# One fixed order per engine for the beginning of a hybrid decoder layer, and w_out and the residual loads moved ahead at the end

## The chip, the cores and the metric

The kernel runs on one core of a Trainium2 chip. The metric is the device time of one execution in microseconds (us), here the median of several runs. A core has TensorE (PE in the profile; its weight loads are PEld), VectorE (DVE), ScalarE (ACT), GpSimd (POOL) and SyncE (SP). DMAs are issued from the queues of SP and ACT.

## The reference

One decoder layer on x of shape (1, 1024, 1024), float32. Two token mixers run side by side on the same normalised input and are merged by gates:

```python
h    = rms_norm(x, pre_w)                      # x * rsqrt(mean(x*x) + EPS) * w
proj = h @ w_in                                # 1024 x 6152
sb_qkv, sb_gate, gdn_qkv, gdn_gate, gdn_a, gdn_b, merge_sb, merge_gdn = split(proj)
o_sb = stick_breaking_attention(q, k, v) * silu(sb_gate)        # 8 heads of 64
gdn_qkv = silu(causal_depthwise_conv(gdn_qkv, conv_w))          # 4 taps
o_g  = rms_norm(gated_delta_rule_chunked(q, k, v, g, beta)) * silu(gdn_gate)   # 4 heads of 128
merged = sigmoid(merge_sb) * (o_sb @ w_branch_sb) + sigmoid(merge_gdn) * (o_g @ w_branch_gdn)
y    = merged @ w_out
out  = x + rms_norm(y, post_w)
```

## The kernel before

Tokens are cut into 8 tiles of 128 (`NT`), the model width into 8 blocks of 128 (`NK`), and the tokens also into 4 quarters of 256 (`QT`) and 2 halves of 512 (`HT`). To keep float32 accuracy every large product is made of three matmuls: each operand is split into a rounded part (`hi`, a ScalarE cast) and the rest (`lo`, a DVE subtraction), and hi x hi, hi x lo and lo x hi add up in PSUM (`dense_mm`, L211; `dense`, L221). A weight block is thus loaded to `raw`, cast to `whi` (L88) and subtracted to `wlo` (L89).

The order of the instructions of each engine is set when the program is built: a scheduler takes instructions by their place in the source as they become ready by its own estimate of times, places the semaphores, and gives out buffers. On the chip each engine then works through its queue in that order and waits where an operand isn't there. `tc.issue_after(i)` puts an instruction behind `i` in its engine's queue. `sp` is a pool of 25 slots of 128 x 1024 float32 that nearly all large tiles share (`slot`); a load into a slot waits until the slot's last reader is done.

*Beginning.* SP loads x_0, x_1, the weight block k0, x_2, x_3, block k1, and x_4 to x_7 (L103, L82). For each token tile `stats` squares it with its sum (ScalarE, L183 or L186), takes the root (L154), and DVE makes the reciprocal root with one step of Newton and scales the tile in place (L155 to L160, L188). For each quarter TensorE transposes two tiles into PSUM (`xT`, L274), ScalarE evicts with the norm weight as `h_hi` (L282), DVE as `h_lo` (L283), and the first two weight blocks (k0, k1) are multiplied with that quarter into `pre0` (L211, copied at L294). `keep_awake` issues matmuls of ones as filler. Only the squares are held in order, each behind the root of the tile before, and two of the weight splits; the rest is the scheduler's order. Behind it come the decay and beta logits (`ab`, L307 and L308), the delta-rule mixer and the attention.

*Attention.* `weave` runs one head pair's attention beside the projections of the next pair (for the last pair, beside merge gates), with side work chosen by planned costs. Then `drain(fill(16), att)` issues what is left of both.

*Merge.* The attention outputs are split into hi and lo (L909, L910). For each of 8 blocks m and both halves TensorE makes `d_ya` (12 matmuls of 512 columns), DVE multiplies it by the gate (L948), GpSimd adds the other branch (L949), and `split_m` casts the sum to `m_hi` (ScalarE, L933) and subtracts to `m_lo` (DVE, L934). The gate `sA` and the other branch `mBl` are loaded back from DRAM (L942, L944). In blocks 4 to 7 the first half of w_out is also loaded and split (`rawo`, L918; L924, L925).

*End.* `y` is made for output half n = 0, then n = 1, tile by tile (L977). The second half of w_out is loaded during n = 0. In n = 1 each tile's residual x is loaded again (`xr`, L990), the tile is squared (L981), the root taken, and two scale-and-adds on DVE (L995) are followed by two stores (L996).

Of the kernel before, what the change touches and what calls it, by code (L numbers as in the profile page):

```python
# [26 lines left out]
def tile_stickbreak_gdn_hybrid(  # L27
# [70 lines left out]
    xs = []  # L98
    raw0 = []
    first = [(2560, "k0"), (2688, "k1")]  # L100
    for t in range(NT):
        xt = slot(f"x_{t}")
        nc.sync.dma_start(xt, x2[t * P:(t + 1) * P, :])  # L103
        xs.append(xt)
        if t in (1, 3):
            c0, nm = first[t // 2]
            raw0.append(load_raw(win[:, c0:c0 + P], NK, nm))
    wab = const.tile([P, NK, 8], F32, name="wab")
    nc.scalar.dma_start(wab, win[:, 4096:4104].rearrange("(k p) c -> p k c", p=P))
    alog = const.tile([P, H], F32, name="alog")  # L110
    nc.scalar.dma_start(alog, a_log.broadcast_to([P, H]))
    dtb = const.tile([P, H], F32, name="dtb")
    nc.scalar.dma_start(dtb, dt_bias.broadcast_to([P, H]))
# [60 lines left out]
    prev_sq = [None]  # L174

    def stats(q):
        for j in range(2):
            t = 2 * q + j
            junk = slot(f"xj_{t}")
            ssx = small.tile([P, 1], F32, tag="ssx", name="ssx")  # L180
            rx = small.tile([P, 1], F32, tag="rx", name="rx")
            if prev_sq[0] is None:
                nc.scalar.activation(junk, xs[t], AF.Square, accum_out=ssx)  # L183
            else:
                with tc.issue_after(prev_sq[0].ins):
                    nc.scalar.activation(junk, xs[t], AF.Square, accum_out=ssx)  # L186
            prev_sq[0] = rsqrt_act(rx, ssx, 1.0 / D, epsb, EPS)
            last = nc.vector.tensor_scalar(xs[t], xs[t], rx, None, op0=ALU.mult)  # L188
        return last

    sc0 = stats(0)
    behind = [(prev_sq[0], sc0)]

    par_ps = gps("par_ps")
    nc.tensor.transpose(par_ps[:, :57], stage, ident[:57, :57])
    par = const.tile([P, 57], F32, name="par")
    with tc.issue_after(sc0.ins):
        nc.vector.tensor_copy(par, par_ps[:, :57])
# [65 lines left out]
    w0 = []  # L264
    pre0 = [slot("pre_k0"), slot("pre_k1")]
    for q in range(4):
        if q < 3:
            stats(q + 1)
        for k2 in range(NK // 2):
            ps = gps(f"xT_{q}_{k2}")  # L270
            for kk in range(2):
                for j in range(2):
                    k = k2 * 2 + kk
                    xt_ = nc.tensor.transpose(ps[:, (kk * 2 + j) * P:(kk * 2 + j + 1) * P],  # L274
                                        xs[2 * q + j][:, k * P:(k + 1) * P], ident)
            if q == 0 and k2 % 2:
                keep_awake(6, xt_)
            qs = slice(q * QT, (q + 1) * QT)
            for kk in range(2):
                k = k2 * 2 + kk  # L280
                pk = ps[:, kk * QT:(kk + 1) * QT]
                ev = nc.scalar.mul(h_hi[:, k, qs], pk, prew[:, k:k + 1])  # L282
                lo_ = nc.vector.scalar_tensor_tensor(h_lo[:, k, qs], pk, prew[:, k:k + 1],  # L283
                                                     h_hi[:, k, qs].bitcast(F32), op0=ALU.mult, op1=ALU.subtract)
        if q < 2:
            act_, dve_ = behind[q]
            with tc.issue_after(act_.ins), tc.issue_after(dve_.ins):
                w0.append(split_w(raw0[q], NK, first[q][1]))
            behind.append((ev, lo_))
        todo = [(0, q)] if q < 2 else ([(1, 0), (1, 1), (0, 2), (1, 2)] if q == 2 else [(0, q), (1, q)])  # L290
        for i, qq in todo:
            ps = psd.tile([P, QT], F32, tag="d", name=f"d_{first[i][1]}_{qq}")
            dense_mm(ps, w0[i], NK, hk, qq * QT, (qq + 1) * QT)
            nc.scalar.copy(pre0[i][:, qq * QT:(qq + 1) * QT], ps)  # L294
# [604 lines left out]
    for p in range(NP):  # L899
        side = chain(*[f(p + 1) for f in stages], fill(1)) if p + 1 < NP else fill(4)  # L900
        weave(until_none(att), 24.0, side, 52.0 if p + 1 < NP else 41.0)
    drain(fill(16), att)


    os_hi, os_lo = [], []
    for p in range(NP):
        hi = slot(f"oshi_{p}", F32R)
        lo = slot(f"oslo_{p}", F32R)
        nc.scalar.copy(hi, osb[p])  # L909
        nc.vector.tensor_sub(lo, osb[p], hi.bitcast(F32))  # L910
        os_hi.append(hi)
        os_lo.append(lo)
# [15 lines left out]

    m_hi = big.tile([P, NK, T], F32R, tag="big", name="m_hi")
# [7 lines left out]
    for m in range(NK):  # L937
        wb = load_w(w_branch_sb[0][:, m * P:(m + 1) * P], 4, f"wbs{m}")
        if m >= 4:
            rw = load_wo(0, m - 4)  # L940
# [12 lines left out]
        if m >= 4:  # L953
            split_wo(0, m - 4, rw)
# [6 lines left out]
    ys, sy0 = [], [None] * NT  # L961
    for n in range(2):
        ns = slice(n * HT, (n + 1) * HT)
        for t in range(NT):
            ts_ = slice(t * P, (t + 1) * P)
            if n == 0:
                if t % 2 == 0:
                    split_wo(1, t // 2, load_wo(1, t // 2))
                ys.append(slot(f"y_{t}"))
            y = ys[t]  # L970
# [18 lines left out]
            xt = slot(f"xr_{t}")  # L989
            nc.sync.dma_start(xt, x2[ts_, :])  # L990
            ry = small.tile([P, 1], F32, tag="ry", name="ry")
            rsqrt_act(ry, ss, 1.0 / D, sy0[t], sy0[t])
            for m in range(2):
                ms = slice(m * HT, (m + 1) * HT)
                nc.vector.scalar_tensor_tensor(y[:, ms], y[:, ms], ry, xt[:, ms], op0=ALU.mult, op1=ALU.add)  # L995
                nc.sync.dma_start(out2[ts_, ms], y[:, ms])  # L996
# [28 lines left out]
```

## Time and profile before

| what | us |
|---|---|
| median of 3 runs | 953.26 (953.21 to 953.89) |
| the profiled execution | 953.58 |
| its span, first to last instruction | 951.8 |
| TensorE busy | 924.6 (97%) |
| DVE busy | 591.0 (62%) |
| ScalarE busy | 384.9 (40%) |
| GpSimd busy | 166.4 (17%) |

Times in the rows are from the span's start. A timeline row has the start, the duration, engine, line, operation, what is written from what, and a count; where a row merges several instructions the duration runs from the first to the last. In square brackets stands how long the engine was idle before it and what released it.

### The profile page before, as it was taken

The page shows a single profiled execution, that of the slowest core. Times are in us where ns is not written, and L with a number is a line of the kernel's source. Part 1 is how long each engine was busy: PE and PEld are TensorE (multiplying, and loading weights), DVE is VectorE, ACT ScalarE, POOL GpSimd, SP SyncE. Part 2 cuts the span into 40 slices and gives each one's busy share as a digit, 9 for nine tenths or more (in the row PEclk, how much of TensorE's full clock was granted, in tenths as well). Part 3 has the DMA queues.
Part 4 walks back from the last instruction along what each step waited for, and adds up shares of the span by engine and source line. Part 5 has one row for each costly group of instructions (what it writes and reads, how often), then busy time and mean ns, then how long its engine had stood idle before and what let it go on. Part 6 is the DMA issues. An engine that isn't in the chain of part 4 may idle for free.

```text
span 951.8 us, 13464 instructions
## 1 busy us (share of the span) xinstructions
PE 924.6 (97%) x5194; PEld 760.5 (80%) x5194; DVE 591.0 (62%) x1066; ACT 384.9 (40%) x861; POOL 166.4 (17%) x113
## 2 busy tenths in 40 slices
PE   8999999999999999999999999999999999989995
PEld 7978888788787888887888788887877877768884
DVE  5669895366999834655576445763774664653244
ACT  6666431145554122442354234543453443232211
POOL 1021210001113000000143112431431450440000
PEclk9999999999999999999999999999999999999998
DMA  7014214300232331006620111121102113761054
GB/s 253 16 45 122 78 67 133 67 23 23 67 78 74 127 93 41 12 12 232 222 67 23 45 54 36 27 64 26 42 23 89 34 40 128 254 232 45 22 177 155
DMA packets 88419, 80.13 MB, mean 84 GB/s; under 512 B 17097, under 2 KB 74530, under 8 KB 88354
## 3 DMA queue, kind: packets, MB, share of 16 engines
q1 hardware_dynamic: 86944, 79.20, 27.0%
q8 instruction: 41, 0.67, 0.3%
q10 hardware_dynamic: 1410, 0.07, 0.1%
q14 instruction: 24, 0.20, 0.1%
HBM read 60.88 MB, written 18.37 MB: 83 GB/s over the span
## 4 chain that ended last, share of the span: by engine, by line
PE 81%; DVE 9%; DMA 4%; ACT 2%; issue 2%; POOL 2%; SPq 0%; DVEq 0%; POOLq 0%; ACTq 0%
PE d_mg L221 17%; PE y L977 6%; PE d_sk L221 5%; PE d_sv L221 5%; PE d_gg L221 5%; PE d_sgt L221 5%; PE d_yb L221 4%; PE d_sq L221 4%; PE d_v L221 4%; PE av L832 4%; PE aT L819 3%; PE d_k L221 2%; PE d_k L211 2%; DMA xr<-in_x_dram 2%; PE z L796 2%
## 5 line engine op out<-in xcount | busy, mean ns | idle before, releaser
L803 POOL TENSOR_TENSOR bt<-bt,kp 128x127 f32<-128x127 f32 (+3 forms) x64 | 102.6, 1613 | 380.6 <-DMA mb<-mg_d 155.4
L802 DVE TENSOR_TENSOR_SCAN kp<-kp,mscan 128x128 f32<-128x128 f32 (+3 forms) x64 | 103.8, 1640 | 26.3 <-ACT kp L799 26.0
L221 PE MATMUL d_mg<-h_hi,whi_mg 128*128 128x512 f32 x256 | 101.5, 396 | 1.0 <-ACT mg L676 1.0
L221 PE MATMUL d_mg<-h_lo,whi_mg 128*128 128x512 f32 x256 | 99.9, 390 | 0.0
L221 PE MATMUL d_mg<-h_hi,wlo_mg 128*128 128x512 f32 x256 | 99.8, 390 | 0.0
L799 ACT ACTIVATE kp<-z 128x384 f32<-128x384 f32 (+4 forms) x96 | 48.5, 505 | 44.3 <-PE z L797 41.5
L221 PEld LDWEIGHTS d_mg<-h_hi,whi_mg 128*128 128x128 f32 x256 | 48.1, 188 | 12.5 <-issue 1.7
L221 PEld LDWEIGHTS d_mg<-h_hi,wlo_mg 128*128 128x128 f32 x256 | 48.1, 188 | 10.2
L221 PEld LDWEIGHTS d_mg<-h_lo,whi_mg 128*128 128x128 f32 x256 | 48.1, 188 | 9.3
L977 PE MATMUL y<-wohi,m_hi 128*128 128x512 f32 (+1 forms) x136 | 51.3, 377 | 0.5 <-ACT m_hi L933 0.5
L977 PE MATMUL y<-wohi,m_lo 128*128 128x512 f32 (+1 forms) x136 | 51.3, 377 | 0.0
L977 PE MATMUL y<-wolo,m_hi 128*128 128x512 f32 (+1 forms) x136 | 51.2, 377 | 0.0
L800 ACT ACTIVATE bt<-z 128x384 f32<-128x384 f32 (+4 forms) x96 | 49.1, 512 | 2.1 <-DMA mB_d<-mb 1.7
L369 POOL TENSOR_TENSOR acc_k<-acc_k,pre_k 128x1024 f32<-128x1024 f32 x4 | 9.6, 2390 | 166.0 <-ACT pre_k L368 166.0
L832 PE MATMUL av<-aT,svn 128*64 128x256 f32 (+1 forms) x320 | 36.8, 366 | 1.1 <-DVE aT L825 1.1
L819 PE MATMUL aT<-ident,bt 128*128 128x128 f32 x288 | 36.5, 273 | 0.0
L89 DVE TENSOR_TENSOR wlo_mg<-raw_mg,whi_mg 128x1024 fp32r<-128x1024 f32 x16 | 24.6, 1535 | 18.7 <-ACT whi_mg L88 18.6
L819 PEld LDWEIGHTS aT<-ident,bt 128*128 128x128 f32 x288 | 32.9, 140 | 3.4 <-issue 0.2
L949 POOL TENSOR_TENSOR sA<-sA,mBl 128x512 f32<-128x512 f32 x16 | 26.2, 1643 | 51.6 <-DVE sA L948 49.5
L981 ACT ACTIVATE yj<-y 128x512 f32<-128x512 f32 (+1 forms) x17 | 9.7, 573 | 61.9 <-PE y L977 53.8
L832 PEld LDWEIGHTS av<-aT,svn 128*64 128x64 f32 x320 | 20.7, 136 | 15.8 <-issue 4.9
L676 ACT ACTIVATE mg<-d_mg 128x512 f32<-128x512 f32 x32 | 19.1, 602 | 31.0 <-PE d_mg L221 28.3
(379 smaller groups left out, 2446.8 us busy)
## 6 DMA issues: line engine op xcount, KB each, us to landing
raw_mg<-in_w_in_dram SPq DMA_DIRECT2D x16, 512.0 KB, 4.4
mg_d<-mg SPq DMA_DIRECT2D x16, 512.0 KB, 3.0
x<-in_x_dram SPq DMA_DIRECT2D x8, 512.0 KB, 6.9
mb<-mg_d SPq DMA_DIRECT2D x8, 512.0 KB, 6.2
mB_d<-mb SPq DMA_DIRECT2D x8, 512.0 KB, 3.7
sA<-mg_d SPq DMA_DIRECT2D x8, 512.0 KB, 5.8
mBl<-mB_d SPq DMA_DIRECT2D x8, 512.0 KB, 5.4
rawo<-in_w_out_dram SPq DMA_DIRECT2D x8, 512.0 KB, 6.7
```

Source lines behind the costliest of these rows:

```text
L89: nc.vector.tensor_sub(lo[:, :nk], raw[:, :nk], hi[:, :nk].bitcast(F32))
L211: nc.tensor.matmul(ps, lhsT=a[:, k], rhs=b[:, c0:c1], start=(k == 0 and i == 0), stop=(k == nk - 1 and i == 2))
L221: nc.tensor.matmul(ps, lhsT=a[:, k], rhs=b[:, hs], start=(k == 0 and i == 0), stop=(k == nk - 1 and i == 2))
L676: nc.scalar.activation(gt[:, hs], ps, AF.Sigmoid)
L799: nc.scalar.activation(kp[:, os_], ps[:, :pc], AF.Sigmoid, scale=-0.125)
L800: nc.scalar.activation(bt[:, os_], ps[:, :pc], AF.Sigmoid, scale=0.125)
L802: nc.vector.tensor_tensor_scan(kp[:, :n], kp[:, :n], mscan[:, :n], 1.0, op0=ALU.mult, op1=ALU.max)
L803: nc.gpsimd.tensor_tensor(bt[:, 1:n], bt[:, 1:n], kp[:, 0:n - 1], op=ALU.mult)
L819: nc.tensor.transpose(ps[:, (a * 2 + j) * P:(a * 2 + j + 1) * P], at[p, a, qb][:, off:off + P], ident)
L832: nc.tensor.matmul(av[a * 64:(a + 1) * 64, j0 * P:2 * P], lhsT=vn[:, c, a * 64:(a + 1) * 64], rhs=aT[:, a * 2 + j0:a * 2 + 2], start=(c == ...
L949: nc.gpsimd.tensor_tensor(ga[:, hs], ga[:, hs], mb[:, hs], op=ALU.add)
L977: nc.tensor.matmul(ps, lhsT=a[:, k, ts_], rhs=b[:, c0:c1], start=(k == 0 and i == 0), stop=(k == NK - 1 and i == 2))
```

## The change

It has four parts.

1. The loads at the start: x_2 is issued on ScalarE's queue, x_3 and k1 follow on SP, and wab, alog and dtb go from ScalarE's queue to SP's, behind x_7.
2. The beginning gets one order for each of ScalarE and DVE: `queued` puts every instruction behind the last one given to that engine. The statistics are cut into a ScalarE part (`stat_act`) and a DVE part (`stat_dve`), and so are the splits of k0 and k1. Squares of tiles 3 to 7 come behind evictions of h: the tiles of the next quarter are squared and scaled between the evictions of this one. k0 and k1 are multiplied with every quarter in turn. One of two bursts of filler among the first transposes is dropped.
3. The first half of w_out is loaded and split ahead of `drain(fill(16), att)` instead of in blocks 4 to 7 of the merge.
4. In the end the residual tile t + 4 is loaded when tile t of n = 1 begins, and the very last store goes through ScalarE's queue.

The core of the diff:

```diff
-    for t in range(NT):
-        xt = slot(f"x_{t}")
-        nc.sync.dma_start(xt, x2[t * P:(t + 1) * P, :])
-        xs.append(xt)
-        if t in (1, 3):
-            c0, nm = first[t // 2]
-            raw0.append(load_raw(win[:, c0:c0 + P], NK, nm))
+    load_tile(0, nc.sync)
+    load_tile(1, nc.sync)
+    load_first(0, nc.sync)
+    load_tile(2, nc.scalar)
+    load_tile(3, nc.sync)
+    load_first(1, nc.sync)
+    for t in range(4, NT):
+        load_tile(t, nc.sync)
...
-    nc.scalar.dma_start(wab, win[:, 4096:4104].rearrange("(k p) c -> p k c", p=P))
+    nc.sync.dma_start(wab, win[:, 4096:4104].rearrange("(k p) c -> p k c", p=P))
...
+    def queued(eng, f):
+        with ExitStack() as held:
+            if eng in tail:
+                held.enter_context(tc.issue_after(tail[eng].ins))
+            tail[eng] = f()
...
+    def stat_act(t):
+        junk = slot(f"xj_{t}")
+        ssx[t] = const.tile([P, 1], F32, name=f"ssx_{t}")
+        rx[t] = const.tile([P, 1], F32, name=f"rx_{t}")
+        queued("act", lambda: nc.scalar.activation(junk, xs[t], AF.Square, accum_out=ssx[t]))
+        queued("act", lambda: nc.scalar.activation(rx[t], ssx[t], AF.Sqrt, scale=1.0 / D, bias=epsb))
...
+    stat_act(0)
+    stat_act(1)
+    split_act(0)
+    stat_act(2)
+    stat_dve(0)
...
+    queued("dve", lambda: nc.vector.tensor_copy(par, par_ps[:, :57]))
+    stat_dve(1)
+    split_dve(0)
...
-            if q == 0 and k2 % 2:
+            if q == 0 and k2 == NK // 2 - 1:
                 keep_awake(6, xt_)
...
+    def x_h(q, banks, k):
+        qs = slice(q * QT, (q + 1) * QT)
+        pk = banks[k // 2][:, (k % 2) * QT:(k % 2 + 1) * QT]
+        queued("act", lambda: nc.scalar.mul(h_hi[:, k, qs], pk, prew[:, k:k + 1]))
+        queued("dve", lambda: nc.vector.scalar_tensor_tensor(h_lo[:, k, qs], pk, prew[:, k:k + 1],
+                                                             h_hi[:, k, qs].bitcast(F32),
+                                                             op0=ALU.mult, op1=ALU.subtract))
...
+    for q in range(4):
+        banks = x_t(q)
+        for k in range(NK):
+            x_h(q, banks, k)
+            if q < 3 and k == 2:
+                if q:
+                    stat_act(2 * q + 2)
+                stat_dve(2 * q + 2)
+            if q < 3 and k == 4:
+                stat_act(2 * q + 3)
+            if q < 3 and k == 5:
+                stat_dve(2 * q + 3)
+        if q == 0:
+            split_act(1)
+            split_dve(1)
+        first_d(0, q)
+        first_d(1, q)
...
+    for k2 in range(4):
+        split_wo(0, k2, load_wo(0, k2))
     drain(fill(16), att)
...
-        if m >= 4:
-            rw = load_wo(0, m - 4)
...
-        if m >= 4:
-            split_wo(0, m - 4, rw)
...
+    def load_x(upto):
+        for t in range(len(xr), min(upto, NT)):
+            xt = slot(f"xr_{t}")
+            nc.sync.dma_start(xt, x2[t * P:(t + 1) * P, :])
+            xr.append(xt)
...
+            else:
+                load_x(t + 4)
...
-            xt = slot(f"xr_{t}")
-            nc.sync.dma_start(xt, x2[ts_, :])
+            xt = xr[t]
...
-                nc.sync.dma_start(out2[ts_, ms], y[:, ms])
+                (nc.scalar if last and m else nc.sync).dma_start(out2[ts_, ms], y[:, ms])
```

`stat_dve` holds the six DVE instructions of one tile's statistics in the order of before (scaled sum, reciprocal, three of the Newton step, the scaling of the tile), `x_t` the 16 transposes of a quarter, `first_d` the 24 matmuls of one block with one quarter and the copy of the result.

## Rows read from the trace of the kernel before

**Rows 1.** The page: busy time of each engine with its share of the span and its instructions, and the chain that ended last by engine.

```profile
PE 924.6 (97%) x5194; PEld 760.5 (80%) x5194; DVE 591.0 (62%) x1066; ACT 384.9 (40%) x861; POOL 166.4 (17%) x113
...
PE 81%; DVE 9%; DMA 4%; ACT 2%; issue 2%; POOL 2%; SPq 0%; DVEq 0%; POOLq 0%; ACTq 0%
```

**Rows 2.** The table by stretch: from and to, length, busy us of TensorE, of its weight loads, of DVE, ScalarE and GpSimd (each with its count), the granted TensorE clock as a share of full speed, the busy share of the DMA engines, and GB/s.

```profile
14.30:22.30 8.00, 6.51 (x40) 5.06 (x40) 6.42 (x18) 5.85 (x14) 0.00 (x0) 1.00 0.67 236
22.30:46.60 24.30, 24.26 (x201) 23.95 (x202) 15.97 (x49) 16.09 (x42) 0.00 (x0) 1.00 0.08 23
46.60:801.70 755.10, 749.73 (x4278) 612.20 (x4276) 493.38 (x849) 318.29 (x718) 136.17 (x80) 1.00 0.24 69
801.70:856.90 55.20, 49.78 (x214) 39.43 (x214) 34.64 (x43) 17.55 (x27) 24.01 (x15) 1.00 0.59 215
...
940.10:951.80 11.70, 0.00 (x0) 0.00 (x0) 3.89 (x10) 0.77 (x3) 0.00 (x0) 0.65 0.45 161
```

**Rows 3.** The chain that ended last, in order of time: start, us, what.

```profile
4.59 5.87 DMA x<-in_x_dram
...
30.60 8.16 PE d_k L211 x68
38.76 1.75 PE xT L274 x16
...
943.64 3.69 DMA xr<-in_x_dram
```

**Rows 4.** The timeline of TensorE, at 22 us, at 46 us and at the first tile of y.

```profile
22.32 0.39 PE L211 MATMUL d_k<-h_hi,whi_k 128*128 128x256 f32 x1 [0.35 <-ACT h_hi L282]
...
46.43 0.40 PE L307 MATMUL ab<-h_hi,wab_r 128*16 128x512 f32 x1
...
856.89 0.50 PE L977 MATMUL y<-wohi,m_hi 128*128 128x512 f32 x1 [0.55 <-ACT m_hi L933]
```

**Rows 5.** The timeline of ScalarE and of DVE in the beginning.

```profile
4.63 1.06 ACT L183 ACTIVATE xj<-x 128x1024 f32<-128x1024 f32 x1 [1.71 <-DMA x<-in_x_dram]
6.01 1.04 ACT L186 ACTIVATE xj<-x 128x1024 f32<-128x1024 f32 x1
...
11.60 1.03 ACT L88 CAST whi_k<-raw_k 128x1024 fp32r<-128x1024 f32 x1
13.78 0.45 ACT L282 ACTIVATE h_hi<-xT,par 128x256 fp32r<-128x256 f32 x1
...
6.13 0.16 DVE L156 RECIPROCAL rx<-rx 128x1 f32<-128x1 f32 x1 [0.17 <-ACT rx L154]
7.70 0.15 DVE L156 RECIPROCAL rx<-rx 128x1 f32<-128x1 f32 x1
...
39.74 2.93 DVE L283 SCALAR_TENSOR_TENSOR h_lo<-xT,par,h_hi 128x256 fp32r<-128x256 f32 x7 [5.15 <-ACT h_hi L282]
```

**Rows 6.** What TensorE waited for in the whole span: us in total, times, longest.

```profile
PE d_ya L221 <- DVE wlo_wbs L89: 3.8, 2, 1.9
```

**Rows 7.** The timeline of DVE and GpSimd in the merge stage: the first and the last multiply (L948), one add beside wlo_wbs, and one turn of the loop.

```profile
806.42 0.69 DVE L948 TENSOR_TENSOR sA<-sA,d_ya 128x512 f32<-128x512 f32 x1 [0.94 <-PE d_ya L221]
...
821.99 1.67 POOL L949 TENSOR_TENSOR sA<-sA,mBl 128x512 f32<-128x512 f32 x1 [2.06 <-DVE sA L948]
...
832.59 0.68 DVE L948 TENSOR_TENSOR sA<-sA,d_ya 128x512 f32<-128x512 f32 x1
833.40 1.28 POOL L949 TENSOR_TENSOR sA<-sA,mBl 128x512 f32<-128x512 f32 x1 [2.11 <-DVE sA L948]
835.37 0.69 DVE L934 TENSOR_TENSOR m_lo<-sA,m_hi 128x512 fp32r<-128x512 f32 x1 [2.10 <-ACT m_hi L933]
835.98 0.68 DVE L948 TENSOR_TENSOR sA<-sA,d_ya 128x512 f32<-128x512 f32 x1
836.58 1.22 DVE L925 TENSOR_TENSOR wolo<-rawo,wohi 128x1024 fp32r<-128x1024 f32 x1
836.74 2.17 POOL L949 TENSOR_TENSOR sA<-sA,mBl 128x512 f32<-128x512 f32 x1 [2.06 <-DVE sA L948]
...
857.48 0.68 DVE L948 TENSOR_TENSOR sA<-sA,d_ya 128x512 f32<-128x512 f32 x1
```

**Rows 8.** The timeline of ScalarE and DVE behind the last matmul.

```profile
940.41 0.19 ACT L981 ACTIVATION_READ_ACCUMULATOR yj<-y 128x1 f32 x1
...
943.10 0.42 DVE L986 TENSOR_TENSOR y<-y,postw 128x256 f32<-128x256 f32 x1
944.19 0.16 DVE L160 TENSOR_TENSOR ry<-ry,rat 128x1 f32<-128x1 f32 x1
947.42 1.42 DVE L995 SCALAR_TENSOR_TENSOR y<-y,ry,xr 128x512 f32<-128x512 f32 x2 [3.07 <-DMA xr<-in_x_dram]
```

**Rows 9.** What the DMA engines moved from 0 to 24 us, in 40 equal slices of 0.6 us.

```profile
GB/s 0 0 6 178 177 348 389 431 358 333 314 216 81 111 314 424 396 379 351 344 332 383 403 403 410 423 403 403 394 339 317 258 130 3 0 0 0 23 125 253
```

**Rows 10.** The loads of k0 and k1: issue durations in ns, first and last start in us, and us from issue to landing.

```profile
L82 SPq DMA_DIRECT2D raw_k<-in_w_in_dram x2: 426/430/433, 1.7 to 6.3; - x2
...
DMA to landing us min/median/max: 6.3/6.3/6.3
```

**Rows 11.** The table by stretch, with the columns of rows 2, ahead of the merge stage.

```profile
784.30:794.50 10.20, 10.20 (x50) 8.10 (x50) 0.04 (x1) 1.22 (x3) 0.00 (x0) 1.00 0.25 79
794.50:801.70 7.20, 7.20 (x69) 5.68 (x65) 6.45 (x10) 5.09 (x7) 0.00 (x0) 1.00 0.79 287
```

## What the change was predicted to do

> **What bounds the kernel now.** The page comes first: TensorE is busy for 97% of the span, and 81% of the chain that ended last runs through it [rows 1]. So a change pays only where TensorE stands still or does filler. The table by stretch says where that is [rows 2]. From 22.3 to 46.6 us it is busy for 24.26 of 24.30 us, and from 46.6 to 801.7 us for all but 5.4 of 755 us. Three stretches are left, and they are those that the diff edits: the first 22 us, 801.7 to 856.9 us (5.4 us idle), and the 11.7 us behind the last matmul.
>
> *The beginning.* TensorE's useful work before 22.32 us is 32 transposes and 24 matmuls of 256 columns. By long runs in the chain (16 transposes in 1.75 us, so 0.11 us each; 68 matmuls in 8.16 us, so 0.12 us each [rows 3]) that is 3.5 + 2.9 = 6.4 us of 22.3. From 22.32 us to the first `ab` matmul at 46.43 us it runs through [rows 4]. The chain shows why it starts late: x_2 is issued at 4.59 us, when x_0 has landed, and lands 5.87 us later, at 10.46 [rows 3]; behind it ScalarE squares it, casts whi_k0, squares x_3, and only at 13.78 us evicts the first h_hi [rows 5].
>
> *The merge stage (L936 to L956).* Two TensorE waits of 1.9 us are put down to wlo_wbs [rows 6]. But TensorE is not alone there. For each half of a block DVE multiplies, GpSimd adds, ScalarE casts and DVE subtracts, and DVE's queue has that subtraction ahead of the next multiply. So a half is a loop of four steps: multiply at 832.59 us, add at 833.40, subtract at 835.37 when the cast is there, next multiply at 835.98, together 3.39 us [rows 7]. TensorE, with 214 matmuls in 49.78 busy us [rows 2], needs 12 x 0.233 = 2.8 us for a half. Its last wait there, at 856.89 us, is for m_hi, the loop's product [rows 4].
>
> *The end.* xr_7 is issued at 943.64 us and takes 3.69 us [rows 3]; the last two scale-and-adds start at 947.42 us, waiting for it, though their factor ry was ready at 944.19 + 0.16 = 944.35 [rows 8].
>
> **The change part by part.** The sum is made against the profiled execution, 953.58 us (its span of 951.8 us and 1.8 around it); the median shown is 953.26.
>
> *Loads at the start.* x_2 moves to ScalarE's DMA queue; wab, alog and dtb move behind x_7 on SP, and their first readers stand behind the last h_hi. Fewer loads are then issued ahead of x_2 and x_3, so they need not wait for x_0 and x_1 to land. The transfers themselves hardly gain: 314 to 431 GB/s move in nearly every slice from 3 to 18 us, with one dip to 216, 81 and 111 GB/s between 6.6 and 8.4 us [rows 9], which the small loads moved away would leave. x_2 now runs beside x_1 and k0. 512 KB at about 400 GB/s are 1.3 us, so k0, which is issued at 1.7 us and lands 6.3 later, at 8.0 [rows 10], comes at 8.0 (the dip that goes pays for x_2) to 9.3 us (it does not).
> The Trainium skill, *DMA: Bandwidth & Descriptors*, section "Issuing engines are not separate DMA queues", speaks against this edit: DMAs from any engine's queue run interleaved on the same 16 DMA engines, and a second issuing engine saves only issue time. By that rule alone k0 comes at the late end, 9.3 us, and the sum below would be 0.7 us worse.
>
> *One order.* ScalarE's queue is now: squares 0 and 1, cast whi_k0, square 2, then the eight h_hi, with square 3 behind the fifth. From k0's landing it takes the cast 1.03, a square with its root 6.01 - 4.63 = 1.38, and h_hi 0.45 [rows 5], together 2.9 us: first h_lo at 10.9 us, or 12.2 with the late k0, or 12.3 if x_2 comes no earlier than 10.46 us. I take 11.5. From there DVE's queue holds 8 h_lo of (2.93 - 0.47)/6 = 0.41 us, two statistics of 7.70 - 6.13 = 1.57 us [rows 5] and the subtraction wlo_k1, 1.2 us like that of wolo [rows 7]: 3.3 + 3.1 + 1.2 = 7.6 us, so wlo_k1 is done at 19.1 us (18.5 to 19.9). By then TensorE has done what it had done at 22.32 us, 24 matmuls and 32 transposes, with the same 168 and 32 left. That is 3.2 us won (2.4 to 3.8). Behind it DVE needs 3.3 + 3.1 = 6.4 us a quarter and TensorE 16 x 0.11 + 48 x 0.12 = 7.5, so TensorE paces; but the last two h_lo of a quarter stand behind a statistic, for which I allow 0.5 us (0 to 1.5). **Beginning: 2.7 us won (0.9 to 3.8).** What follows shifts whole, since TensorE has no idle in the 24 us behind it and 5.4 in the next 755 [rows 2]. The dropped filler (6 of 12 keep-awake matmuls among the transposes) costs nothing while the clock holds; else it is a rival below.
>
> *w_out ahead.* Four loads, four casts and four subtractions of 1.22 us [rows 7] leave the merge stage and go behind the last attention weave. They are free if they come before 794.5 us: of the 10.2 us from 784.3 on DVE is busy 0.04 and ScalarE 1.22 [rows 11]. From 794.5 to 801.7 us DVE is busy 6.45 of 7.2 us [rows 11], and all four subtractions there cost up to 4 x 1.22 = 4.9 us. The 12 tiles need slots of the 25; I count 11 held at 785 us (4 bt, svn, 4 osb, up to 2 gates), so they fit. In the merge stage the waits for wlo_wbs (3.8 us [rows 6]) can go, yet the loop of four stays: an add beside wolo takes 2.17 us, one beside nothing 1.28, and one beside wlo_wbs alone 1.67 (at 821.99 us) [rows 7], so a removed wolo gives about 0.5 us, for three of them 1.5. **Merge: 1.5 us won.** Bounds: every half by the loop, with the slower add in every second, is 15 x (3.39 + 0.2) = 53.9 us against 857.48 - 806.42 = 51.1 from first to last multiply [rows 7], 2.8 lost; TensorE alone pacing, 5.4 won, its idle there [rows 2]. I lean to the loop: nothing in the diff reorders it.
>
> *Residual loads ahead.* xr_7 is issued with tile 4 instead of behind the stores of tile 6. ScalarE's last read ends at 940.41 + 0.19 = 940.60 us; from the multiply by postw to ry's end it is 943.10 to 944.35, 1.25 us; so the scale-and-adds start at 940.65 + 1.25 = 941.9 instead of 947.42 us [rows 8]. **End: 5.5 us won** (5.0 to 5.7). The cover is three tiles of matmuls between load and use; slots are free, since the first half of w_out ends with the last matmul of n = 0. The last store on ScalarE's queue gains nothing by itself: its half is ready 0.7 us behind the other's.
>
> Sum: 953.58 - 2.7 - 1.5 - 5.5 = **943.9 us**.
>
> **The rivals.**
> *The beginning gives nothing.* The fixed queues wait in order, so a late k0 or x_3 holds every eviction behind it, and an order of TensorE's that puts k1's matmuls ahead of the next transposes would leave DVE idle. For it: two whole engines are chained. Against it: the loads move at 400 GB/s and end by 19 us [rows 9], ahead of their turn. Time: 953.6 - 1.5 - 5.5 = 946.6.
> *The clock falls.* In its first 8 us of real work TensorE gets transposes, one burst of filler, and then matmuls at DVE's pace. At half rate the 24 matmuls and 16 transposes cost 2.9 + 1.8 = 4.7 us more: 948.6. Against it: the clock was 1.00 through the same sparse stretch, 14.30 to 22.30 us [rows 2], though with two bursts ahead.
> The Trainium skill, *TensorE: Matmul & The Clock Gate*, section "Part 4: PE-mode transpose", says that transposes do not count as the array's activity in the way matmuls do; by that rule this rival gains, and no row here separates the two.
> *The merge stage opens.* If the new order has the next multiply ahead of the subtraction, TensorE paces: 943.9 - (5.4 - 1.5) = 940.0.
> *Slower: SP's queue blocks.* If 12 slots are free only when the last bt are transposed (about 798 us), the four w_out loads stand at the head of SP's in-order queue, and mg_d, raw_wbs, sA and mBl wait behind them: 4 x 1.3 us of transfers, then four subtractions in the busy stretch, 5.2 + 4.9 = 10.1 us, against 2.7 + 5.5 won elsewhere: 955.5. It decides once the loads are issued after about 796 us; issued by 788 they cost nothing. Against it: the last weave has no next head pair to prepare, which frees some 8 slots.
> *The subtractions alone in the busy stretch:* 943.9 + 4.9 = 948.8.
>
> **How the numbers follow.** Chances: forecast 0.62; beginning gives nothing 0.10; clock 0.06; merge opens 0.08; subtractions late 0.09; SP blocks 0.05. The forecast's own range by its bounds is 940 to 947.5; to leave out no more than 2 in 10 the range goes on to the 948.8 above and to an opened merge stage with the beginning's better end below: 939 to 949. The three runs of this kernel lie within 0.1%, so 0.2% (1.9 us) is about what can be told from no change. Faster 0.93, within 0.2% 0.03, slower 0.04.
>
> **What would show it.** The first `ab` matmul near 43.7 us (now 46.43), the first d_k matmul near 11.5 us, and no 3 us wait for x_2's square; in the merge stage no wlo_wbs waits, but m_hi still the last to release y; no DMA wait at L995, and the last scale-and-adds less than 2 us behind the last matmul. The prediction is wrong if the 755 us between are scheduled anew with much more than their 5.4 us of idle, or if the w_out splits stand between 794 and 806 us.

## The result and the profile after

The change makes the kernel slower: 960.85 us (median of 4 runs, 959.19 to 961.49) against 953.56 (median of 4 runs beside them, 953.21 to 953.89), a ratio of 1.0079 with a 95% interval of 1.0066 to 1.0092. The forecast was 943.9, with a range of 939 to 949. The span of the profiled execution is 959.2 us, 7.4 more than before. TensorE's starts divide it like this (us; "last z" is the last score matmul of the attention):

| stretch | before | after | difference |
|---|---|---|---|
| start to first `ab` | 46.43 | 50.38 | +3.95 |
| to the first d_mg behind the last z | 728.07 | 729.91 | +1.84 |
| to the first d_ya (attention tail) | 27.12 | 35.62 | +8.50 |
| to the first y (merge stage) | 49.80 | 48.38 | -1.42 |
| to the last matmul | 88.35 | 88.29 | -0.06 |
| to the end | 12.08 | 6.63 | -5.45 |

The page of after, as [rows 1], and the table by stretch, with the columns of [rows 2]:

```profile
PE 930.6 (97%) x5182; PEld 762.2 (79%) x5182; DVE 589.0 (61%) x1066; ACT 385.7 (40%) x861; POOL 166.0 (17%) x113
PE 83%; DVE 8%; ACT 3%; issue 2%; DMA 2%; POOL 1%; SPq 0%; ACTq 0%; DVEq 0%; POOLq 0%
```
```profile
22.40:50.40 28.00, 25.43 (x197) 23.48 (x198) 16.28 (x49) 16.60 (x42) 0.00 (x0) 1.00 0.07 20
50.40:788.00 737.60, 731.98 (x4158) 597.94 (x4155) 486.06 (x838) 312.15 (x709) 137.85 (x80) 1.00 0.23 68
...
800.60:815.90 15.30, 9.45 (x64) 6.97 (x62) 9.34 (x12) 7.05 (x10) 0.00 (x0) 0.78 0.35 115
815.90:864.30 48.40, 45.22 (x195) 35.52 (x193) 25.67 (x36) 13.31 (x21) 19.85 (x13) 1.00 0.62 220
```

From 22.4 us to `ab`, where TensorE had no idle time before, it has 2.6 us; from 800.6 to 815.9 us it is busy for 9.45 of 15.3 us, and part of that at a lower clock.

*The attention tail.* What TensorE waited for from 788 to 816 us, then ScalarE's timeline, then that of SP's queue, and what SP's queue waited for from 776 to 804 us:

```profile
PE aT L869 <- ACT aT L877: 5.9, 1, 5.9
```
```profile
789.79 1.04 ACT L960 CAST wohi<-rawo 128x1024 fp32r<-128x1024 f32 x1
795.88 1.05 ACT L960 CAST wohi<-rawo 128x1024 fp32r<-128x1024 f32 x1 [5.05 <-DMA rawo<-in_w_out_dram]
...
800.19 1.04 ACT L960 CAST wohi<-rawo 128x1024 fp32r<-128x1024 f32 x1
806.29 1.04 ACT L960 CAST wohi<-rawo 128x1024 fp32r<-128x1024 f32 x1 [5.05 <-DMA rawo<-in_w_out_dram]
807.24 1.08 ACT L726 ACTIVATE mg<-d_mg 128x512 f32<-128x512 f32 x2
808.21 1.08 ACT L877 COPY aT<-aT 128x512 f32<-128x512 f32 x2
```
```profile
775.83 0.45 SPq L954 DMA_DIRECT2D rawo<-in_w_out_dram  x1
789.92 0.34 SPq L727 DMA_DIRECT2D mg_d<-mg  x1
790.36 0.38 SPq L82 DMA_DIRECT2D raw_wbs<-in_w_branch_sb_dram  x1
790.79 1.51 SPq L954 DMA_DIRECT2D rawo<-in_w_out_dram  x2
801.04 0.37 SPq L82 DMA_DIRECT2D raw_wbs<-in_w_branch_sb_dram  x1
801.50 1.64 SPq L954 DMA_DIRECT2D rawo<-in_w_out_dram  x1
```
```profile
SPq L727 <- ACT mg L726: 13.6, 1, 13.6
SPq L82 <- DVE sgT L889: 9.0, 1, 9.0
SPq L954 <- PE aT L869: 1.5, 1, 1.5
```

The four loads do not go out together. In SP's queue the second and third stand behind the store of a merge gate (`mg_d`), which waits 13.6 us for ScalarE's sigmoid, until 789.92 us. The fourth stands behind the load of raw_wbs, which waits some 9 us for DVE, until 801.04; its own slot costs it 1.5 us more (for TensorE's transposes of a bt), so that it leaves at 803.0. Its cast stands in ScalarE's queue ahead of two sigmoids of mg and the copies of aT, so ScalarE stands for 5.05 us and TensorE for 5.9. Behind that wait TensorE runs at half its clock (1.2 GHz) for 6.8 us; the table by stretch before, during and behind it:

```profile
789.00:802.70 13.70, 13.70 (x75) 11.23 (x74) 5.31 (x6) 4.45 (x6) 0.00 (x0) 1.00 0.45 143
802.70:807.10 4.40, 0.29 (x3) 0.05 (x1) 0.00 (x0) 0.81 (x1) 0.00 (x0) 1.00 0.47 155
807.10:813.90 6.80, 5.05 (x24) 3.59 (x26) 6.07 (x8) 5.60 (x9) 0.00 (x0) 0.50 0.19 77
```

5.05 busy us at half the clock are 2.5 more than at the full one (an estimate); with the wait of 5.9 that is 8.4 of the 8.50.

*The beginning.* The first d_k comes at 12.26 us instead of 14.28, 0.8 later than the forecast 11.5. Then ScalarE and DVE wait for each other. Their timelines at the end of the beginning, and one row of ScalarE in the kernel before:

```profile
44.30 0.85 ACT L317 ACTIVATE h_hi<-xT,par 128x256 fp32r<-128x256 f32 x2
45.74 0.84 ACT L317 ACTIVATE h_hi<-xT,par 128x256 fp32r<-128x256 f32 x2 [0.58 <-DVE h_lo L318]
```
```profile
44.83 0.88 DVE L318 SCALAR_TENSOR_TENSOR h_lo<-xT,par,h_hi 128x256 fp32r<-128x256 f32 x2 [1.31 <-ACT h_hi L317]
46.25 0.88 DVE L318 SCALAR_TENSOR_TENSOR h_lo<-xT,par,h_hi 128x256 fp32r<-128x256 f32 x2 [0.54 <-ACT h_hi L317]
```
```profile
42.70 0.47 ACT L282 ACTIVATE h_hi<-xT,par 128x256 fp32r<-128x256 f32 x1 [0.66 <-DVE h_lo L283]
```

A pair of columns takes 1.42 us (44.83 to 46.25), 0.71 a column; before, seven h_lo ran back to back at 0.41 [rows 5]. Two columns share a PSUM bank, one of the separate blocks of PSUM, in which a quarter's transposes land, and the h_hi of a bank's second column waits 0.58 us for DVE's h_lo of its first. The kernel before had the same wait: 0.66 us at 42.70 us, where two columns of one bank came in turn. The Trainium skill, *PSUM — Partial Sum Buffer*, section "PSUM bank collisions raise a hardware error", has a rule that accounts for it: two engines must not access one bank at once, reads against reads included, and the compiler back end's scheduler puts a dependency between them. The trace agrees, with the 0.58 us.

*The merge stage and the end.* DVE at two turns of the loop, and DVE behind the last matmul:

```profile
848.43 0.68 DVE L998 TENSOR_TENSOR sA<-sA,d_ya 128x512 f32<-128x512 f32 x1
...
851.55 0.69 DVE L986 TENSOR_TENSOR m_lo<-sA,m_hi 128x512 fp32r<-128x512 f32 x1 [1.84 <-ACT m_hi L985]
852.16 0.68 DVE L998 TENSOR_TENSOR sA<-sA,d_ya 128x512 f32<-128x512 f32 x1
854.95 0.69 DVE L986 TENSOR_TENSOR m_lo<-sA,m_hi 128x512 fp32r<-128x512 f32 x1 [2.11 <-ACT m_hi L985]
855.56 0.68 DVE L998 TENSOR_TENSOR sA<-sA,d_ya 128x512 f32<-128x512 f32 x1
...
954.54 0.16 DVE L168 TENSOR_TENSOR ry<-ry,rat 128x1 f32<-128x1 f32 x1
954.73 1.41 DVE L1051 SCALAR_TENSOR_TENSOR y<-y,ry,xr 128x512 f32<-128x512 f32 x2
```

The loop of four steps is still there, 3.40 us from multiply to multiply [rows 7]. What went are the slow turns: those with a subtraction of w_out took 4.23 us before (835.98 to 840.21 us), and such a turn takes 3.73 now (848.43 to 852.16). At the end the scale-and-adds follow ry without the DMA wait of [rows 8].

### The profile page after: what moved, and what is told of

Same layout as the page of the kernel before. It is cut to its first block, busy times and chain, and to the rows that moved or that the text cites. A ratio compares the mean times of both kernels' runs of the same rounds, so it can differ in the third digit from the quotient of the medians.

```text
span 959.2 us, 13456 instructions
## 1 busy us (share of the span) xinstructions
PE 930.6 (97%) x5182; PEld 762.2 (79%) x5182; DVE 589.0 (61%) x1066; ACT 385.7 (40%) x861; POOL 166.0 (17%) x113
## 4 chain that ended last, share of the span: by engine, by line
PE 83%; DVE 8%; ACT 3%; issue 2%; DMA 2%; POOL 1%; SPq 0%; ACTq 0%; DVEq 0%; POOLq 0%
PE d_mg L255 17%; PE y L1034 8%; PE d_sk L255 5%; PE d_sv L255 5%; PE d_gg L255 5%; PE d_sgt L255 5%; PE d_yb L255 4%; PE d_v L255 4%; PE d_sq L255 4%; PE av L882 4%; PE aT L869 3%; PE d_k L255 2%; PE d_ya L255 2%; PE z L846 2%; PE z L847 2%
## 5 line engine op out<-in xcount | busy, mean ns | idle before, releaser
L853 POOL TENSOR_TENSOR bt<-bt,kp 128x127 f32<-128x127 f32 (+3 forms) x64 | 104.7, 1646 | 378.6 <-DMA mb<-mg_d 155.4
L255 PEld LDWEIGHTS d_mg<-h_hi,wlo_mg 128*128 128x128 f32 x256 | 48.0, 188 | 10.2
L999 POOL TENSOR_TENSOR sA<-sA,mBl 128x512 f32<-128x512 f32 x16 | 23.7, 1482 | 60.2 <-DVE sA L998 60.2
L1034 PEld LDWEIGHTS y<-wohi,m_hi 128*128 128x128 f32 x136 | 25.6, 188 | 7.1 <-DVE sA L998 1.7
```

The lines of the kernel that those rows point to most:

```text
L255: nc.tensor.matmul(ps, lhsT=a[:, k], rhs=b[:, hs], start=(k == 0 and i == 0), stop=(k == nk - 1 and i == 2))
L853: nc.gpsimd.tensor_tensor(bt[:, 1:n], bt[:, 1:n], kp[:, 0:n - 1], op=ALU.mult)
L999: nc.gpsimd.tensor_tensor(ga[:, hs], ga[:, hs], mb[:, hs], op=ALU.add)
L1034: nc.tensor.matmul(ps, lhsT=a[:, k, ts_], rhs=b[:, c0:c1], start=(k == 0 and i == 0), stop=(k == NK - 1 and i == 2))
```

## The experiments

Each run stands beside runs of the kernel before (medians 953.2 to 953.9 us). "Tail" is from the first d_mg behind the last z to the first d_ya, "merge" from there to the first y; the expectations of u_wo and u_split_late count the tail from a later d_mg (19.4 us where this count has 27.1). All ratios are to the kernel before.

| kernel | us | ratio, 95% interval | first d_k | first ab | tail | merge |
|---|---|---|---|---|---|---|
| before | 953.56 | | 14.28 | 46.43 | 27.12 | 49.80 |
| after | 960.85 | 1.0079 (1.0066 to 1.0092) | 12.26 | 50.38 | 35.62 | 48.38 |
| u_wo | 952.17 | 0.9985 (0.9976 to 0.9994) | 12.29 | 50.25 | 27.11 | 49.87 |
| u_split_late | 952.86 | 0.9988 (0.9978 to 0.9997) | 12.55 | 50.64 | 27.12 | 49.46 |
| u_two | 950.81 | 0.9974 (0.9960 to 0.9987) | 12.82 | 50.13 | 27.11 | 49.27 |
| u_bank | 955.94 | 1.0030 (1.0019 to 1.0042) | 12.05 | 46.43 | 35.78 | 48.38 |
| u_bank_stat | 956.15 | 1.0024 (1.0013 to 1.0035) | 12.14 | 45.52 | 35.41 | 48.38 |
| u_wo_free | 956.74 | 1.0037 (1.0023 to 1.0052) | 23.59 | 53.90 | 27.12 | 50.73 |
| b_end | 949.22 | 0.9947 (0.9931 to 0.9964) | 15.40 | 48.69 | 27.12 | 50.13 |
| u_wo_merge | 947.22 | 0.9933 (0.9913 to 0.9952) | 12.92 | 51.03 | 27.11 | 43.84 |
| b_end_merge | 942.48 | 0.9887 (0.9872 to 0.9901) | 14.28 | 46.39 | 27.12 | 43.82 |
| u_best | 941.39 | 0.9877 (0.9854 to 0.9901) | 12.99 | 46.39 | 27.12 | 43.83 |
| u_best_two | 942.47 | 0.9886 (0.9871 to 0.9901) | 12.34 | 46.55 | 27.11 | 43.75 |
| u_best_sp | 941.02 | 0.9869 (0.9854 to 0.9883) | 12.42 | 44.82 | 27.11 | 43.86 |

**The attention tail: u_wo, u_split_late, u_two.** First the whole part undone, then only its casts and subtractions put back, then half of it.

```
u_wo: loads and splits in the merge stage again
-    for k2 in range(4):
-        split_wo(0, k2, load_wo(0, k2))
...
+        if m >= 4:
+            rw = load_wo(0, m - 4)
...
+        if m >= 4:
+            split_wo(0, m - 4, rw)
u_split_late: loads as in the change, splits in the merge stage
-    for k2 in range(4):
-        split_wo(0, k2, load_wo(0, k2))
+    rws = [load_wo(0, k2) for k2 in range(4)]
...
+        if m >= 4:
+            split_wo(0, m - 4, rws[m - 4])
u_two: two blocks behind the weave, two in merge blocks 6 and 7 as in u_wo
-    for k2 in range(4):
+    for k2 in range(2):
```

> The changed kernel with only the w_out part undone: the four loads and splits of the first half of w_out stand in merge blocks 4 to 7 again, the beginning and the end are the changed ones. In the changed kernel the stretch from the first d_mg behind the last weave to the first d_ya is 8.5 us longer than before, and there ScalarE's queue holds a cast of w_out that waits for its load ahead of the copies of aT. Theory 1 (this part alone makes the loss there): the 8.5 us go, the 1.4 us that the merge stage won go too, 960.85 - 8.5 + 1.4 = 953.8 us, and the stretch is 19.4 us again. Rival (the stretch is longer because the beginning changed the state in which it is entered): still 960 us or above.

> The changed kernel with the four w_out loads still issued behind the last weave, but their casts and subtractions back in merge blocks 4 to 7. It tells apart what in the moved part costs 8.5 us. Theory 1a (ScalarE's in-order queue stands at a cast of w_out whose load is late): the stretch from the first d_mg behind the weave to the first d_ya returns to about 19.4 us, the time to 953 to 955 us. Theory 1b (SP's in-order queue stands at a w_out load that waits for a slot, so that mg's weights and stores come late): the stretch stays near 28 us and the time near 960 us. Between the two: each has its share.

> The changed kernel with two of the four w_out blocks split ahead behind the last weave and the other two loaded and split in merge blocks 6 and 7: 6 tiles instead of 12 want slots in the attention tail. Theory 1c (the casts wait because the pool has no slots for twelve tiles until TensorE has transposed the last bt): six fit, the casts run before 795 us, the tail is 27.1 us from the first d_mg behind the last z as before, and the time is 952 to 953.5 us. Rival (a cast ahead of the copies of aT costs that wherever it stands, slots or not): two of the four waits remain and the time is 955 us or more.

u_wo has the tail of before to 0.01 us and 952.17 us, 1.6 less than expected: this part costs 8.7 us net, and the beginning has no share in the tail. u_split_late is there too, with loads that go out earlier than in the change (three issued by 775.5 us, the last at 789.7). So loads ahead are harmless; with the chain of rows above (TensorE waits for a copy of aT, ScalarE stands at a cast, the cast waits for its load), the casts in ScalarE's queue do the harm. u_two shows on what that depends. Its ScalarE, its SP queue, and its tail with the columns of [rows 2]:

```profile
787.88 1.04 ACT L960 CAST wohi<-rawo 128x1024 fp32r<-128x1024 f32 x1
793.30 1.05 ACT L960 CAST wohi<-rawo 128x1024 fp32r<-128x1024 f32 x1 [4.38 <-DMA rawo<-in_w_out_dram]
```
```profile
788.00 0.34 SPq L727 DMA_DIRECT2D mg_d<-mg  x1
...
788.87 0.90 SPq L954 DMA_DIRECT2D rawo<-in_w_out_dram  x1
```
```profile
786.20:805.50 19.30, 19.30 (x122) 15.35 (x122) 9.58 (x13) 9.32 (x13) 0.33 (x1) 1.00 0.47 153
```

ScalarE still stands at a cast for 4.38 us, but at a time when TensorE wants nothing of it, and TensorE is busy throughout. So a cast that waits is not costly in itself: it is when its load comes as late as 801 us. The time, 950.81 us, is 1.2 below the range that theory 1c gave, and the theory (slots) is not shown: with six tiles, too, the second load stands behind the store of mg_d and goes out at 788.87 us, about as late as with twelve (790.79), and the only wait of a w_out load for a slot in the rows of the change is the 1.5 us of the fourth. What made the loads late is their place in SP's queue, between stores and loads that wait for ScalarE and DVE. Why the scheduler placed them there stays open; it may be the slots by its own estimate, since in all three kernels the load that would need a fourth slot for w_out (cast and rest counted) goes out only at 788.9 to 790.8 us.

**The beginning: u_bank, u_bank_stat, u_wo_free.**

```
u_bank, in x_t and x_h:
-                k = k2 * 2 + kk
+                k = k2 + kk * (NK // 2)
-    pk = banks[k // 2][:, (k % 2) * QT: ...]
+    pk = banks[k % (NK // 2)][:, (k // (NK // 2)) * QT: ...]
u_bank_stat: also stat_act(4), stat_act(5) behind split_act(1); stat_act(6), stat_act(7) in q == 1
u_wo_free: u_wo, and in queued():
-            held.enter_context(tc.issue_after(tail[eng].ins))
```

> The changed kernel with one edit in the beginning: a PSUM bank holds the transposed columns k and k + 4 of a quarter instead of k and k + 1; the orders of the queues stay as they are. Theory 2 (ScalarE's eviction of k + 1 waits for VectorE's subtraction of k because both read one bank, so a pair costs 1.42 us instead of 0.82): evictions run at 0.41 to 0.47 us each, 2.4 us less for a quarter where they pace; the first ab matmul comes at 50.4 - 4 to 50.4 - 7, that is 43.5 to 46.5 us, and the time falls to 954 to 957 us. Rival (the late landing of k0 and x_3, or the order of the transposes on TensorE, sets the pace): first ab within 1 us of 50.4, the time within 1 us of 960.9.

u_bank did what theory 2 says: first `ab` at 46.43, 3.95 us earlier, and 955.94 us, 4.9 less. The bank pairs cost the 3.95 us, then; the loads and the order of the queues are the same. Its ScalarE and DVE in the first quarter run without waits between columns, 0.36 and 0.40 us from one to the next:

```profile
11.52 1.92 ACT L317 ACTIVATE h_hi<-xT,par 128x256 fp32r<-128x256 f32 x5
```
```profile
12.01 1.27 DVE L318 SCALAR_TENSOR_TENSOR h_lo<-xT,par,h_hi 128x256 fp32r<-128x256 f32 x3 [0.52 <-ACT h_hi L317]
...
18.27 1.22 DVE L220 TENSOR_TENSOR wlo_k<-raw_k,whi_k 128x1024 fp32r<-128x1024 f32 x1
```

From its first h_lo to the end of wlo_k1 DVE takes 7.5 us (12.01 to 19.49), where the prediction had added up 7.6; in the change it takes 9.9. Yet the first `ab` is only that of before, although the 24th d_k matmul and the 32nd transpose have begun by 19.6 us, and before by 21.7. ScalarE, DVE and TensorE show the next stall:

```profile
22.52 0.37 ACT L325 COPY pre_k<-d_k 128x256 f32<-128x256 f32 x1 [2.39 <-PE d_k L245]
22.80 1.06 ACT L196 ACTIVATE xj<-x 128x1024 f32<-128x1024 f32 x1
```
```profile
23.98 0.15 DVE L203 TENSOR_SCALAR ray<-ssx 128x1 f32<-128x1 f32 x1 [3.30 <-ACT xj L196]
```
```profile
25.95 0.33 PE L307 MATMUL xT<-ident,x 128*128 128x128 f32 x1 [0.76 <-DVE x L208]
```

The copies of pre_k are not in the fixed order, and one stands ahead of the square of tile 4 and waits for TensorE.

> The changed kernel with columns k and k + 4 in one PSUM bank and one more edit: ScalarE's squares of tiles 4 to 7 stand a quarter earlier in its queue (tiles 4 and 5 behind the cast of whi_k1, 6 and 7 in the second quarter). With the bank edit alone the first ab matmul came at 46.43 us and the time was 955.94; there ScalarE waited 2.39 us for TensorE at a copy of pre_k that stands ahead of the square of tile 4, and TensorE later 0.76 and 0.60 us for the scaled tiles of the third and fourth quarter, each at the head of a stall of 1.2 and 0.8 us. Theory 3 (the squares come a quarter too late, because they stand behind copies that wait for TensorE): first ab at 44 to 45 us, time 953.5 to 954.5. Rival (the stalls are the dependence of d_k on each h_lo, and the tiles' scaling only shows first): first ab within 0.5 us of 46.4, time within 0.7 us of 955.9.

Inconclusive. In the profile the stalls at 25 and 34 us are gone and `ab` comes at 45.52, 0.9 us earlier, less than the 1.4 to 2.4 expected; the median, 956.15, doesn't show it. So the place of the squares is at most a part of that stall, and the rest has no cause shown.

> The changed kernel with the w_out part undone (952.17 us; first d_k at 12.29, first ab at 50.25) and without the fixed orders: same instructions and loads, but the scheduler places ScalarE's and VectorE's. It puts both casts of whi_k first, so ScalarE waits for k1 and the first d_k comes late, at 16 to 19 us; behind that it alternates the banks (xT_0, 1, 0, 2, 1, 3). Theory 2 (what costs is the order 0 to 7 through two columns of one bank): from the first d_k to the first ab 29 to 31 us instead of 38.0, first ab at 46 to 49 us although the start is 4 to 6 us later, time 949 to 952. Rival (the rewritten beginning costs by its loads and its late start, not by the order): first ab at 54 us or later, time above 955.

From the first d_k to the first `ab` it takes 30.3 us instead of 38.0, as theory 2 has it, but first `ab` (53.90) and time (956.74) are those of the rival. The scheduler, left alone, starts d_k only at 23.59 us, with TensorE at half its clock on the way. The two stretches:

```profile
13.40:23.50 10.10, 6.00 (x27) 5.65 (x28) 8.89 (x32) 7.85 (x20) 0.00 (x0) 0.50 0.81 230
23.60:53.90 30.30, 30.06 (x242) 28.74 (x242) 16.81 (x52) 18.41 (x46) 0.00 (x0) 1.00 0.01 2
```

The run does not separate the two. By 23.6 us seven h_hi of the first quarter and four squares beyond those of tiles 0 and 1 are done, so TensorE can run through (30.06 of 30.30 us) whatever the order of banks. That the banks cost the 3.95 us is shown by u_bank; this run shows what the fixed order gives, the early start.

**The end and the merge loop: b_end, u_wo_merge.**

```
b_end: load_x and the store on ScalarE's queue, put into the kernel before
u_wo_merge, in split_m:
-        nc.vector.tensor_sub(m_lo[:, m, hs], ...)
+        with tc.issue_after(after.ins):      # the multiply of the next half
+            nc.vector.tensor_sub(m_lo[:, m, hs], ...)
```

> The kernel before with only the last part of the change: the residual loads are issued from tile 4 of the second half on, the last store on ScalarE's queue. Behind the last matmul the changed kernel has 6.35 us instead of 11.75. Theory (that part stands by itself): 953.56 - 5.4 = 948.2 us. Rival (the loads issued earlier take the place of something in the y stage, or the gain hangs on the other parts): above 950 us.

The end is 6.62 us instead of 12.08, 5.46 won. The median shows 4.3, 1 us short of the theory. Its runs spread from 947.99 to 952.46; the slowest is the profiled one, in which two half-clock stretches fell (below). What the other three had is not known.

> The changed kernel with the w_out part undone (952.17 us) and one edit in the merge stage: VectorE's subtraction of a half is issued behind the multiply of the next half. Theory 4 (multiply, add, cast and subtraction are a loop because the subtraction stands ahead of the next multiply): a half costs TensorE's 2.8 us, the stage from the first d_ya to the first y falls from 49.87 to 45 to 46 us, the time to 947.5 to 948.5. Rival (GpSimd's add and the loads of mBl set the pace anyway): the stage within 1 us of 49.9, the time within 1 us of 952.2.

Theory 4 held, with more than expected: the stage falls by 6.0 us, and TensorE has no idle time left in it. From the first y to the last matmul it is 1.1 us shorter, too (87.23 for 88.35). The stage in u_wo and in u_wo_merge:

```profile
805.70:855.50 49.80, 44.90 (x194) 35.72 (x193) 31.49 (x41) 16.15 (x24) 20.93 (x14) 1.00 0.67 240
```
```profile
808.00:851.80 43.80, 43.80 (x194) 36.07 (x193) 29.94 (x41) 16.48 (x25) 19.76 (x14) 1.00 0.74 269
```

**Together: u_best, b_end_merge, u_best_two, u_best_sp.** u_best is u_wo with the edits of u_bank_stat and u_wo_merge; b_end_merge is b_end with u_wo_merge's edit; u_best_two has u_two's w_out; u_best_sp issues x_2 on SP's queue.

> All that was found in one kernel: the changed kernel with the w_out part undone, columns k and k + 4 in one PSUM bank, the squares a quarter earlier, and the merge stage's subtraction behind the next multiply. If the parts add up: 952.17 - 3.9 (bank) - 2 (squares) - 4.4 (merge) = 941.9 us. If the stages share one gain (the merge stage or the beginning gives its part back later): 945 us or more. The kernel before with the end part alone has 949.2.

> The kernel before with the end part and with the merge stage's subtraction behind the next multiply; its beginning is the old one. It tells what the mended beginning of the best kernel (941.39 us) is worth against the old one. If the mended beginning gives what its first ab in the profiles says (46.4 against 46.43 us, nothing): 941 to 943 us. If the forecast's 2.7 us are there after all: 944 us. If merge and end share a gain: 946 us or more.

> The best kernel (941.39 us) with two of the four w_out blocks split ahead behind the last weave, as in the run that came 1.4 us below the one with none ahead. There TensorE still waited for the merge loop; here the loop is open and the stage without idle time (0.0 us), so theory: no gain from moving the splits out of it, 941 to 942 us. Rival (the two splits also delay something else in the stage): 939.5 to 940.5.

> The best kernel (941.39 us) with the load of x_2 on SP's queue behind k0 instead of ScalarE's. In the changed kernel x_2 and k0 land at 9.19 and 9.40 us, k0 1.4 us later than before. If the second queue only shares the transfers: k0 lands at 8 to 8.6 us, x_2 at 9.5 to 10.5, the first d_k 0.5 to 1 us earlier (11.3 to 12.5), and the time 940.5 to 941.4. If it saves waiting in SP's queue: x_2 and with it the second quarter come 1 us later, 942 or above.

The time is as expected, 941.39 against 941.9, 1.2% below the kernel before, but the terms are not, so that is luck. Against u_wo, u_best's first `ab` comes 3.9 us earlier (50.25 to 46.39), as much as the bank edit alone was to give, and the squares' 2 us are not there; the merge edit gives 7.1 (6.0 in its stage, 1.1 behind it) where 4.4 were put. The mended beginning is worth 1.1 us against the old one (941.39 and 942.48), or 1.5 with x_2 on SP's queue; these kernels ran beside different runs of before and the intervals overlap, so even its sign is not sure. With the loop open, early splits give nothing (942.47). In u_best_sp k0 lands 6.4 us after its issue, in u_best, with x_2's load on ScalarE's queue, after 8.4. The last line of the loads of k0 and k1 in u_best and in u_best_sp [rows 10]:

```profile
DMA to landing us min/median/max: 8.4/8.4/8.4
```
```profile
DMA to landing us min/median/max: 6.4/6.4/6.4
```

x_2 itself lands at 9.42 us in u_best and at 9.48 in u_best_sp: the second queue won it nothing. That is the Trainium skill's rule that the prediction weighed (*DMA: Bandwidth & Descriptors*, "Issuing engines are not separate DMA queues"), and these traces agree. How much k0 lost by it is less sure. It took 7.4 to 8.4 us in the ten traces with x_2 on ScalarE's queue, but b_end, with the loads of before, has 8.5 where before has 6.3, and x_2 behind k0 was traced once. The 0.4 us in the time are within the interval.

## Why the prediction was wrong, step by step

The sum with the measured terms: 943.9 + 6.65 (beginning: 3.95 lost for 2.7 won) + 8.50 (tail) + 1.84 (middle) = 960.9, against 960.85.

- **w_out ahead, "free if they come before 794.5 us" and "I count 11 held at 785 us, so they fit": failed, and it cost most.** The step took the four loads as issued together behind the weave and the slots as the only thing that could hold them. They came to issue at 775.8, 790.8, 791.8 and 801.5 us, behind stores and loads that wait in SP's queue; a slot held the last one for 1.5 us. Casts stood at 795.88 and 800.19 us, which is the prediction's own sign of being wrong. The point named in the rival, "once the loads are issued after about 796 us", was right, and the last load passed it. That rival had 0.05 and 955.5 us. Its victims were wrong as well: it had the w_out loads hold up mg_d and raw_wbs in SP's queue, and it was the other way round; and it priced transfers and DVE's subtractions, 10.1 us. What stood behind the waiting instruction on *its own engine*, the mg sigmoids and the aT copies behind ScalarE's cast, was not asked, and it cost 8.5 us with the clock.
- **One order, "h_lo of ... 0.41 us" and "so TensorE paces": failed.** The 0.41 was read where DVE had seven evictions to run through [rows 5]. By the semaphores that its h_hi waited for there (three times TensorE's, then three times DVE's), ScalarE changed banks from one to the next; the new order takes both columns of a bank in turn, and 0.71 us is its price. u_bank gave back all of the 3.95 us. The trace of before had the price, in the 0.66 us at 42.70.
- **First d_k at 11.5: about right.** It came at 12.26; k0 landed at 9.40, the late end, for which the prediction had 12.2.
- **First `ab` near 43.7: no kernel reached it;** the mended ones have 44.8 to 46.6. So even without the bank pairs at most 1.6 of the 2.7 us are there. The 0.5 us that the prediction allows for the statistics left out that squares stand behind copies of pre_k, but moving them gave 0.9 us; the cause of the rest is open.
- **Merge 1.5 us: right** (1.42), with its mechanism: turns with a subtraction of w_out fall from 4.23 to 3.73 us, and the loop stays. An opened loop, put at 5.4 us, gives 6.0 in the stage.
- **End 5.5 us: right** (5.45).
- **"What follows shifts whole": the middle is 1.84 us off, with a half-clock stretch of 3.41 us** in this execution (next section). The eight executions without it there take 728.07 to 728.77 us for the middle, the six with it 729.82 to 730.18, two of these with the old beginning. So up to 0.7 us can be the change's, and the rest goes with the stretch.

## What to carry to other kernels

Before an instruction that waits for a load is moved ahead in an in-order queue, look where that load will stand in its own queue and what holds the entries ahead of it, and list what stands behind the instruction on its own engine: here loads went early without harm when their consumers did not. An eviction's price read from a run in one order holds for that order alone; where two engines read PSUM as here, let consecutive evictions change banks (0.40 us for 0.71 in u_bank). And where a loop over engines closes through one engine's queue order, the order of two instructions there (6 us here) can be worth more than the loads around it.

## What the hardware showed beyond that

Half-clock stretches of TensorE come and go between executions. One of 6.8 us at 0.50 behind the 5.9 us wait was in each of the three kernels that had the wait (after, and u_bank and u_bank_stat with 5.7 and 6.0 us) and in none of the others; in u_bank and u_bank_stat:

```profile
803.95:810.75 6.80, 5.75 (x26) 3.96 (x28) 6.33 (x9) 4.91 (x8) 0.00 (x0) 0.50 0.25 88
```
```profile
800.55:807.35 6.80, 4.36 (x20) 3.24 (x22) 5.38 (x8) 6.08 (x9) 0.00 (x0) 0.50 0.19 77
```

Others do not follow the edit: one of 3.41 us near 260 us in six of the fourteen profiled executions, one of 3.4 to 10.2 us near 16 us in five, both with the old beginning and the new, and one of 3.41 us in the merge stage of u_wo_free. Near 260 us TensorE waits 1.8 to 2.0 us (oT, for DVE) in all fourteen, and in six of them the half clock follows. After is one of these; around that wait it has 0.73 busy us in 2, then the stretch:

```profile
262.30:264.30 2.00, 0.73 (x6) 0.69 (x7) 2.00 (x9) 1.43 (x2) 0.00 (x0) 1.00 0.00 0
264.40:267.80 3.40, 3.40 (x12) 2.62 (x11) 3.40 (x13) 0.95 (x2) 0.00 (x0) 0.50 0.19 29
```

A stretch of 3.4 busy us costs about 1.7 (an estimate from its busy time; the middles above differ by 1.1 to 2.1), as much as the smaller terms of the sum. The near-16 kind is the prediction's rival of a falling clock, which the change's own profile does not have; it came with one burst of filler and, in b_end, with both. So a single profile's first `ab` or middle is uncertain by that much, and medians of some runs are needed below 2 us.
